# Expert weights cut by row blocks instead of by column halves, and the small group's two halves in one go

## The chip, the cores and the metric

The kernel runs on one core of one Trainium2 chip. The metric is the device time of one execution in microseconds, as the median of several runs. Five engines work side by side, each through its own queue in order: TensorE (PE in the profile; PEld is its weight load), VectorE (DVE), ScalarE (ACT), GpSimd (POOL) and SyncE (SP), which issues most DMAs here.

## The reference, cut to what matters

One transformer layer on 1024 tokens of width 1024: differential attention, then a mixture of experts, then a norm. The change lies in the experts. Each token chooses two of 16 experts; for every expert, with `t` the tokens routed to it:

```
hid = silu(t @ w_gate[e]) * (t @ w_up[e])      # w_gate, w_up: 1024 x 512
hid = hid * gates[:, e]
y  += hid @ w_down[e]                          # w_down: 512 x 1024
```

Everything is float32 in and out.

## The kernel before

**Precision.** Every float32 operand of the experts is split into a high part (fp32r, a cast on ScalarE) and a low part (float32 minus high part, a subtraction on VectorE). A product of a full block sums three terms: high x high, high x low and low x high (`TERMS`).

**Pieces of weights.** An expert has `NP = 12` pieces of 128 x 1024 float32 (512 KB): pieces 0 to 7 are gate (even) and up (odd), 8 to 11 are down. A piece of gate or up was four row blocks of 128 by half of the 512 columns. Half `hf` of the 512 hidden columns (256 each) so had its four pieces, `hf * 4` to `hf * 4 + 3`. `load_raw` issues the DMA of a piece into one of 11 raw tiles (`wraw`). `split_piece` does the cast `whi` (L1117) and the subtraction `wlo` (L1122) into a ring of 14 slots, so expert e + 1's piece i + 2 takes the slot of expert e's piece i.

**Order.** The order on TensorE, ScalarE, VectorE and GpSimd is written out by hand: instructions run in the order in which the program issues them. `block(e)` issues one expert. Its first 128 tokens are the full block: 48 gate and up products of half 0 (`gu`, 256 columns each), then 48 of half 1, counted 0 to 95. Between them stand hooks, `(count, what)`: a hook of count c is issued ahead of product c. `SPL` are the hooks that split pieces 6 to 11 of this expert; `later` holds what the expert before has postponed: its small group's last part at count `DSM` = 12, its output `yo` at 60. `gate` makes silu(gate) x up (L1397, L1398), `hid` transposes the result (L1404) and splits it (L1407, L1408), `down` multiplies it with the down pieces, 12 products of 512 columns for each half.

**The small group.** An expert with more than 128 tokens has a second group of up to `M2` = 64. Its work stands in branches, `small(...)`, that each engine takes or skips by the count of tokens; six of the experts (4, 6, 11 to 14) take them in this run. High and low parts lie side by side in one 128-row operand there, so a half takes 32 gate and up products and 8 down products. In order, after the full block's gate of half 1: the transposes of the group's tokens (L1292); full `down` of half 0 with the full block's second `hid` ("h1") in it; splits of pieces 0 and 1 of the next expert; small half 0 and its gate; splits 2 and 3; full `down` of half 1; then `small_c`: transposes and split of small half 0 (`hs`), small half 1 and its gate, small down products of half 0, transposes and split of small half 1; splits 4 and 5; and in the next block, at count 12, `small_d`: the small down products of half 1 (`spy`), the sum and the scatter.

**Block 0** has its own order of splits (`SP0`, and lines 1599 to 1622); there the low parts of pieces 3 and 4 are made by GpSimd. After expert 14 the last scatters and the final norm follow.

Of the kernel before, what the change touches and what calls it, by code (L numbers as in the profile page):

```python
# [4 lines left out]
F32 = mybir.dt.float32  # L5
F32R = mybir.dt.float32r
# [4 lines left out]
OP = mybir.AluOpType  # L11
# [4 lines left out]
P = 128  # L16
# [15 lines left out]
def f(ap):  # L32
    return ap.bitcast(F32)


def build(tc, x, c, ada_w, ada_b, norm_mix, norm_ffn, w_in, lq1, lk1, lq2, lk2, subln, w_out,
          rgw, rgb, rew, reb, wg, wu, wd, norm_final, out, dbg=None):
    nc = tc.nc
# [21 lines left out]
    ident = const.tile([P, P], F32, name="ident")  # L60
# [140 lines left out]
    for t in range(TB):  # L201
# [8 lines left out]
        for kk in range(2):  # L210
# [4 lines left out]
            for i in range(4):  # L215
                k = kk * 4 + i
# [806 lines left out]
    n = 5  # L1023
# [7 lines left out]
    for i, (h, qb) in enumerate(seq):  # L1031
# [6 lines left out]
        n = RATE.get(i, n)  # L1038
# [17 lines left out]
    WP = {}  # L1056
# [16 lines left out]
    M2 = 64  # L1073
# [10 lines left out]
    def load_raw(e, i):  # L1084

        raw = raw_tile()
        if HOLD[0]:

            nc.gpsimd.memset(raw[:, 0:1], 0.0)
        if i < 8:  # L1090
            src = (wg if i % 2 == 0 else wu)[0, e].rearrange("(k p) n -> p k n", p=P)
            hf, kk = i // 4, (i // 2) % 2
            nc.sync.dma_start(raw.rearrange("p (k n) -> p k n", k=4),
                              src[:, kk * 4:kk * 4 + 4, hf * 256:hf * 256 + 256])
        else:
            nc.sync.dma_start(raw, wd[0, e, (i - 8) * P:(i - 7) * P])
        RAW[e, i] = raw
# [39 lines left out]
    def split_to(n):  # L1137
        while nsplit[0] < min(n, NE * NP):
            split_piece(*divmod(nsplit[0], NP))
            split_done(1)  # L1140
# [5 lines left out]
    EVAC = 60  # L1146
    DSM = 12
    N0 = 28
    SPL = [(0, 6), (24, 7), (56, 8), (64, 9), (80, 10), (90, 11)]

    SP0 = [(20, split_hi, 8), (20, split_lo, 8), (30, split_hi, 9), (30, split_lo, 9), (40, split_hi, 10), (40, split_lo, 10),
           (45, split_hi, 11), (45, split_lo, 11)]
# [27 lines left out]
    mp = tc.alloc_tile_pool(name="moe", bufs=1, reuse_waits="tile")  # L1180
    mps = tc.alloc_tile_pool(name="moep", bufs=1, space=PSUM, reuse_waits="tile")

    v = nc.vector
# [117 lines left out]
    def run(g):  # L1301
        try:
            while True:
                next(g)
        except StopIteration as r:
            return r.value
# [68 lines left out]
    def gu_tile(tag="gu"):  # L1375
        return mps.tile([P, 2, 256], F32, name="gu", tag=tag, bufs=2 if tag == "gu" else 1)

    def gu(e, XT, hf, R, tag="gu", pg=None):
        pg = gu_tile(tag) if pg is None else pg
        for k in range(KT):  # L1380
            for xi, wi in TERMS[R]:
                for i in range(2):
                    yield
                    w = WP[e, hf * 4 + (k // 4) * 2 + i][wi].rearrange("p (k n) -> p k n", k=4)
                    nc.tensor.matmul(pg[:, i], XT[:, xi, k], w[:, k % 4], start=(k == 0 and xi == 0 and wi == 0 and i == 0),  # L1385
                                     stop=(k == KT - 1 and (xi, wi) == TERMS[R][-1] and i == 1), skip_group_check=True)
        return pg

    def gate(pg, g, R, lo=None, sl=None):

        sl = mp.tile([P, 256], F32, name="sl") if sl is None else sl
        if R == M2:
            lo = lo[:R].rearrange("p (i n) -> p i n", i=2)
            nc.scalar.copy(lo, pg[R:])
            v.tensor_tensor(lo, lo, pg[:R], op=OP.add)
            pg = lo
        nc.scalar.activation(sl[:R], pg[:R, 0], AF.Silu)  # L1397
        v.scalar_tensor_tensor(sl[:R], sl[:R], g[:R], pg[:R, 1], op0=OP.mult, op1=OP.mult)  # L1398
        return sl

    def hid(sl, R, name="hid", bufs=2, hT=None):
        ph = mps.tile([P, 2, P], F32, name="tp")
        for i in range(2):
            nc.tensor.transpose(ph[:, i, :R], sl[:R, i * P:(i + 1) * P], ident[:R, :R])  # L1404
        hT = mp.tile([P, 2, 2, P], F32R, name=name, bufs=bufs) if hT is None else hT
        hi, lo = (hT[:, 0, :, :R], hT[:, 0, :, R:]) if R == M2 else (hT[:, 0], hT[:, 1])
        nc.scalar.copy(hi, ph[:, :, :R])  # L1407
        v.tensor_tensor(lo, ph[:, :, :R], f(hi), op=OP.subtract)  # L1408
        return hT

    def down(e, py, hf, hT, R, ns=(0, 1)):
        terms = [(i, xi, wi) for i in range(2) for xi, wi in TERMS[R]]
        terms.sort(key=lambda t: t[1])
        for n in ns:
            for j, (i, xi, wi) in enumerate(terms):
                yield
                nc.tensor.matmul(py[n], hT[:, xi, i], WP[e, 8 + hf * 2 + i][wi][:, n * 512:(n + 1) * 512],  # L1417
                                 start=(hf == 0 and j == 0), stop=(hf == 1 and j == len(terms) - 1), skip_group_check=True)
# [72 lines left out]
    def block(e, XT, idx, tt, hooks):  # L1491


        count = [0]
        ix = idx[:, 0:1]
        last = e == NE - 1
        hooks = sorted(hooks, key=lambda hk: hk[0])
        py = [mps.tile([P, 512], F32, name="py%d" % i) for i in range(2)]

        def upto(c):  # L1500
            while hooks and hooks[0][0] <= c:
                hooks.pop(0)[1]()

        def go(g, n=1 << 30):
            try:
                for _ in range(n):
                    next(g)
                    upto(count[0])
                    count[0] += 1
            except StopIteration as r:  # L1510
                return r.value

        s0 = gate(go(gu(e, XT, 0, P)), tt[:, 0, 3:4], P)
        g1 = gu(e, XT, 1, P)
        go(g1, N0)
        h0 = hid(s0, P)
        pg1 = go(g1)
        if last:
            s1 = gate(pg1, tt[:, 0, 3:4], P)
            go(down(e, py, 0, h0, P))  # L1520
            h1 = hid(s1, P)
            nc.scalar.preload_act_table_set("natural_log_exp_and_others")  # L1522
            upto(1 << 30)
            run(down(e, py, 1, h1, P))
            finish15(ix, py, mp.tile([P, D], F32, name="yo"), XC[0])
            tc.no_sync_barrier()
            with tc.If(cnts[e] > P, label="small"):
                small15(XT, idx[:M2, 1:2], tt[:, 1, 3:4])
            tc.no_sync_barrier()
            with tc.If(cnts[NE] > P + M2):  # L1530
                rest(XT)
            return
        upto(199)
        n = cnts[e]
        g = tt[:, 1, 3:4]
        xs = XG[e, 1]

        def small(what):
            tc.no_sync_barrier()
            with tc.If(n > P):  # L1540
                what()

        def splits(k):
            split_to(nsplit[0] + k)

        s1 = gate(pg1, tt[:, 0, 3:4], P)
        pt = small_pt()
        small(lambda: small_evac(small_pe(xs, pt), XT))
        d = down(e, py, 0, h0, P)
        take(d, 9)  # L1550
        h1 = hid(s1, P)
        run(d)
        splits(2)
        sl, hs = mp.tile([P, 256], F32, name="sl"), mp.tile([P, 2, 2, P], F32R, name="hs")
        pg = gu_tile()
        small(lambda: gate(run(gu(e, XT, 0, M2, pg=pg)), g, M2, xs[:, 0:512], sl))
        splits(2)
        run(down(e, py, 1, h1, P))
        pg2 = gu_tile("idx")
        spy = [mps.tile([P, 512], F32, name="spy%d" % n, tag="xt", bufs=2) for n in range(2)]  # L1560

        def small_c():
            hid(sl, M2, hT=hs)
            gate(run(gu(e, XT, 1, M2, pg=pg2)), g, M2, xs[:, 512:1024], sl)
            run(down(e, spy, 0, hs, M2))
            hid(sl, M2, hT=hs)

        def small_d():
            for n in range(2):
                run(down(e, spy, 1, hs, M2, (n,)))  # L1570
                fold(spy, oyo, n)
                r = slice(n * 512, (n + 1) * 512)
                v.tensor_tensor(oyo[:M2, r], oyo[:M2, r], g2b[:M2, r], op=OP.mult)
            scatter_add(idx[:M2, 1:2], oyo[:M2])

        small(small_c)
        splits(2)
        later.append((DSM, lambda: small(small_d)))

        def evac():  # L1580
            yo = mp.tile([P, D], F32, name="yo")
            for n in range(2):
                v.tensor_tensor(yo[:, n * 512:(n + 1) * 512], py[n], g2b[:, n * 512:(n + 1) * 512], op=OP.mult)
            scatter_add(ix, yo)

        later.append((EVAC if e < NE - 2 else 0, evac))
        upto(1 << 30)
# [3 lines left out]
    g = nc.gpsimd  # L1591
    END = [*[(c, lambda: split_to(nsplit[0] + 1)) for c, i in SPL],
           *[(40, norm_load, t) for t in range(TB)], (40, rows15),
# [10 lines left out]
    XT = run(xpose(XG[0, 0]))  # L1604
# [22 lines left out]
    for e in range(NE):  # L1627
        idx, tt = ns[e]
# [42 lines left out]
        if 0 < e < NE - 1:  # L1671
            hooks += [(c, lambda: split_to(nsplit[0] + 1)) for c, i in SPL]
        if e == NE - 2:
# [7 lines left out]
        if e + 1 < NE:  # L1681
# [4 lines left out]
            XT = xp[0]  # L1686
# [34 lines left out]
```

## Time and profile before

| | us |
|---|---|
| median of 3 runs | 1222.99 (1222.16 to 1225.85) |
| the profiled execution's own time | 1222.66 |
| its span, first to last instruction | 1220.8 |
| mean granted TensorE clock | 0.961 |
| PE, DVE, ACT, POOL busy in the span | 1108.1, 939.6, 727.8, 265.2 |

The experts run from about 760 us on, expert 1 at 785, expert 2 at 807. How to read the rows below: a line of the timeline gives start and duration in us, the engine, the line of the kernel, the operation, what it writes and reads by the program's names, how many were merged into the row (x), and in brackets the idle time of the engine before it with what ended it. DVEq and ACTq are the engines' sequencers, L1540 is the skipped or taken branch.

### The profile page before, as it was taken

How to read it: one execution, taken by the hardware profiler on the slowest of the kernel's cores; microseconds unless marked ns; L12 is line 12 of the kernel's file. 1: busy time of each engine (PE TensorE's matmuls, PEld its weight loads, DVE VectorE, ACT ScalarE, POOL GpSimd, SP SyncE). 2: the span in 40 equal slices, each digit the busy share in tenths (PEclk: the TensorE clock that was granted, in tenths of full speed). 3: DMA queues.
4: the chain of work that ended last, by engine and by line, in shares of the span. 5: the costliest groups of instructions: out<-in, count | busy, mean ns of one | idle time of the engine just before them, and what ended most of it. 6: DMA issues, size and time to landing. Idle time of an engine off the chain costs nothing. (4 is left out here: it accounts for less than half of the span.)

```text
span 1220.8 us, 19162 instructions
## 1 busy us (share of the span) xinstructions
PE 1108.1 (91%) x6760; PEld 916.9 (75%) x6760; DVE 939.6 (77%) x1560; ACT 727.8 (60%) x1206; POOL 265.2 (22%) x283
## 2 busy tenths in 40 slices
PE   3889999999999999999889996999999999999961
PEld 3667777777777778787668885887888878888851
DVE  5869788888888777778884557798797989677754
ACT  5565766667666676776674323567465666554543
POOL 3011010111101011114304204343232332222121
PEclk9899999999999999999899996999999999999985
DMA  9722022322332110102417724799888999777645
GB/s 325 216 63 72 23 87 88 100 78 86 96 91 87 44 40 27 43 27 95 138 57 239 255 96 153 242 346 334 272 251 263 294 344 330 239 228 238 200 132 199
DMA packets 153255, 199.55 MB, mean 163 GB/s; under 512 B 12967, under 2 KB 124232, under 8 KB 153138
## 3 DMA queue, kind: packets, MB, share of 16 engines
q1 hardware_dynamic: 146432, 179.86, 45.0%
q0 software_dynamic: 6512, 17.68, 6.0%
q8 instruction: 63, 1.03, 0.4%
q10 hardware_dynamic: 194, 0.54, 0.1%
q14 instruction: 54, 0.44, 0.1%
HBM read 175.77 MB, written 27.67 MB: 167 GB/s over the span
## 5 line engine op out<-in xcount | busy, mean ns | idle before, releaser
L1122 DVE TENSOR_TENSOR wlo<-wraw,whi 128x1024 fp32r<-128x1024 f32 x187 | 224.9, 1231 | 33.2 <-ACT whi L1117 22.9
L1385 PE MATMUL gu<-whi,XT 128*128 128x256 f32 x1216 | 209.2, 284 | 2.7
L1117 ACT CAST whi<-wraw 128x1024 fp32r<-128x1024 f32 x192 | 193.4, 1049 | 6.4 <-ACTq L1540 4.7
L486 ACT ACTIVATE E<-E,mn 128x1024 f32<-128x1024 f32 x128 | 147.1, 1151 | 83.2 <-DVE mn L483 82.9
L1385 PEld LDWEIGHTS gu<-whi,XT 128*128 128x128 f32 x1216 | 172.3, 191 | 10.0 <-issue 5.8
L483 DVE CUSTOM_DVE_ANT_0 E<-S,negd 128x1024 f32<-128x1024 f32 x128 | 152.8, 1219 | 18.7 <-PE S L478 18.1
L1385 PE MATMUL gu<-wlo,XT 128*128 128x256 f32 x704 | 148.1, 289 | 2.0 <-POOL wlo L1122 2.0
L285 PE MATMUL mm<-hH,wh 128*128 128x512 f32 x336 | 139.3, 415 | 2.1 <-DVE V L384 2.1
L285 PE MATMUL mm<-hL,wh 128*128 128x512 f32 x336 | 140.2, 417 | 0.0
L285 PE MATMUL mm<-hH,wl 128*128 128x512 f32 x336 | 138.9, 413 | 0.0
L143 POOL TENSOR_TENSOR wl<-wraw,wh 128x1024 fp32r<-128x1024 f32 x21 | 50.6, 2410 | 325.3 <-ACT wh L142 255.3
L513 ACT CAST aH<-tp 128x512 fp32r<-128x512 f32 x128 | 74.0, 578 | 73.7 <-PE tp L511 73.5
L1385 PEld LDWEIGHTS gu<-wlo,XT 128*128 128x128 f32 x704 | 109.4, 191 | 2.4 <-POOL wlo L1122 2.2
L497 DVE SCALAR_TENSOR_TENSOR E<-E,r 128x1024 f32<-128x1024 f32 x64 | 85.8, 1341 | 27.9 <-ACT E L495 26.3
L514 DVE TENSOR_TENSOR aL<-tp,aH 128x512 fp32r<-128x512 f32 x128 | 88.0, 687 | 17.4 <-ACT aH L513 16.3
L1417 PE MATMUL py<-whi,hid 128*128 128x512 f32 x256 | 93.3, 426 | 3.2 <-ACT hid L1407 0.5
L511 PE MATMUL tp<-ident,E 128*128 128x128 f32 x512 | 79.2, 278 | 10.2 <-DVE aL L514 7.2
L511 PEld LDWEIGHTS tp<-ident,E 128*128 128x128 f32 x512 | 62.8, 142 | 33.5 <-DVE aL L514 13.9
L693 PE MATMUL mm<-wo,wh 128*128 128x512 f32 x240 | 80.1, 408 | 1.3 <-ACT mm L705 1.3
L285 PEld LDWEIGHTS mm<-hH,wh 128*128 128x128 f32 x336 | 63.5, 189 | 18.2 <-issue 5.1
L285 PEld LDWEIGHTS mm<-hH,wl 128*128 128x128 f32 x336 | 63.4, 189 | 17.1 <-issue 7.9
L285 PEld LDWEIGHTS mm<-hL,wh 128*128 128x128 f32 x336 | 63.3, 189 | 16.9 <-issue 8.0
(342 smaller groups left out, 2229.6 us busy)
## 6 DMA issues: line engine op xcount, KB each, us to landing
wraw<-in_expert_w_gate SPq DMA_DIRECT2D x64, 512.0 KB
wraw<-in_expert_w_up SPq DMA_DIRECT2D x64, 512.0 KB
wraw<-in_expert_w_down SPq DMA_DIRECT2D x64, 512.0 KB
aw<-in_ada_w SPq DMA_DIRECT2D x64, 256.0 KB
wraw<-in_attn_w_in SPq DMA_DIRECT2D x23, 512.0 KB
ld<-in_ada_w SPq DMA_DIRECT2D x32, 256.0 KB
ld<-in_x SPq DMA_DIRECT2D x8, 512.0 KB
xt<-in_x SPq DMA_DIRECT2D x8, 512.0 KB
```

The costliest lines, as they stand in the source:

```text
L285: nc.tensor.matmul(pq, w[:, k], t[k][:, n], start=(k == 0 and i == 0), stop=(k == KT - 1 and i == 2))
L483: nc.vector.tensor_tensor_reduce(out=e, in0=sps[m], in1=negd[:, w0:w0 + S], op0=OP.add, op1=OP.min, scale=-slope, scalar=3.0e38, accum_out=mn)
L486: nc.scalar.activation(e, e, AF.Exp, bias=mn, scale=-1.0, accum_out=sm)
L497: nc.vector.scalar_tensor_tensor(es[0], es[1], r2, es[0], op0=OP.mult, op1=OP.add)
L511: nc.tensor.transpose(pt[:, i], a[:, k * P:(k + 1) * P], ident)
L513: nc.scalar.copy(th[:, kk * 4:kk * 4 + 4, q], pt)
L514: nc.vector.tensor_tensor(tl[:, kk * 4:kk * 4 + 4, q], pt, f(th[:, kk * 4:kk * 4 + 4, q]), op=OP.subtract)
L693: nc.tensor.matmul(py, w[:, h], wt[h][:, ns], start=(h == 0 and s == 0), stop=(h == H - 1 and s == 2))
L1117: nc.scalar.copy(WP[e, i][0], RAW[e, i])
L1122: eng.tensor_tensor(low, RAW[e, i], f(high), op=OP.subtract)
L1385: nc.tensor.matmul(pg[:, i], XT[:, xi, k], w[:, k % 4], start=(k == 0 and xi == 0 and wi == 0 and i == 0), stop=(k == KT - 1 and (xi, wi) ...
L1417: nc.tensor.matmul(py[n], hT[:, xi, i], WP[e, 8 + hf * 2 + i][wi][:, n * 512:(n + 1) * 512], start=(hf == 0 and j == 0), stop=(hf == 1 and ...
```

## The change

A gate or up piece is now two row blocks of 128 by all 512 columns. Both halves of the gate and up products so read all eight pieces, two of them (gate and up) for each pair of row blocks. The hook that splits piece 7 moves from count 24 to count 8. In the small group, both halves of the gate and up products come one after the other, each in a branch of its own, with two splits between them and two behind them; the full `down` of half 1 and two more splits follow; `small_c` is now only four transposes with one cast and one subtraction; and all 16 small down products are in `small_d`. The gate's result is written into `xs`, in place, instead of a tile `sl`.

```diff
         if i < 8:
             src = (wg if i % 2 == 0 else wu)[0, e].rearrange("(k p) n -> p k n", p=P)
-            hf, kk = i // 4, (i // 2) % 2
-            nc.sync.dma_start(raw.rearrange("p (k n) -> p k n", k=4),
-                              src[:, kk * 4:kk * 4 + 4, hf * 256:hf * 256 + 256])
+            kk = i // 2 * 2
+            nc.sync.dma_start(raw.rearrange("p (k n) -> p k n", k=2), src[:, kk:kk + 2])
...
-    SPL = [(0, 6), (24, 7), (56, 8), (64, 9), (80, 10), (90, 11)]
+    SPL = [(0, 6), (8, 7), (56, 8), (64, 9), (80, 10), (90, 11)]
...
-                    w = WP[e, hf * 4 + (k // 4) * 2 + i][wi].rearrange("p (k n) -> p k n", k=4)
-                    nc.tensor.matmul(pg[:, i], XT[:, xi, k], w[:, k % 4], start=(k == 0 and xi == 0 and wi == 0 and i == 0),
+                    w = WP[e, k // 2 * 2 + i][wi].rearrange("p (k n) -> p k n", k=2)
+                    nc.tensor.matmul(pg[:, i], XT[:, xi, k], w[:, k % 2, hf * 256:hf * 256 + 256], start=(k == 0 and xi == 0 and wi == 0 and i == 0),
...
         run(d)
+        hs = mp.tile([P, 2, 2, P], F32R, name="hs")
+        pgs = [gu_tile(), gu_tile("idx")]
+
+        def small_b(hf):
+
+            gate(run(gu(e, XT, hf, M2, pg=pgs[hf])), g, M2, xs[:, hf * 512:hf * 512 + 512],
+                 xs[:, hf * 512:hf * 512 + 256])
+
+
+        small(lambda: small_b(0))
         splits(2)
-        sl, hs = mp.tile([P, 256], F32, name="sl"), mp.tile([P, 2, 2, P], F32R, name="hs")
-        pg = gu_tile()
-        small(lambda: gate(run(gu(e, XT, 0, M2, pg=pg)), g, M2, xs[:, 0:512], sl))
+        small(lambda: small_b(1))
         splits(2)
         run(down(e, py, 1, h1, P))
-        pg2 = gu_tile("idx")
+        splits(2)
         spy = [mps.tile([P, 512], F32, name="spy%d" % n, tag="xt", bufs=2) for n in range(2)]
 
         def small_c():
-            hid(sl, M2, hT=hs)
-            gate(run(gu(e, XT, 1, M2, pg=pg2)), g, M2, xs[:, 512:1024], sl)
-            run(down(e, spy, 0, hs, M2))
-            hid(sl, M2, hT=hs)
+            ph = mps.tile([P, 2, P], F32, name="tp").rearrange("p i (h n) -> p (i h) n", h=2)
+            for i in range(4):
+                c = (i // 2) * 512 + (i % 2) * P
+                nc.tensor.transpose(ph[:, i], xs[:M2, c:c + P], ident[:M2, :M2])
+            h = hs.rearrange("p h i n -> p (h i) n")
+            nc.scalar.copy(h[:, :, :M2], ph)
+            v.tensor_tensor(h[:, :, M2:], ph, f(h[:, :, :M2]), op=OP.subtract)
 
         def small_d():
             for n in range(2):
-                run(down(e, spy, 1, hs, M2, (n,)))
+                for hf in range(2):
+                    run(down(e, spy, hf, hs[:, hf:hf + 1], M2, (n,)))
                 fold(spy, oyo, n)
...
         small(small_c)
-        splits(2)
         later.append((DSM, lambda: small(small_d)))
```

## Rows read from the trace of the kernel before

**Rows 1.** The page: busy us, share of the span and instructions.
```profile
PE 1108.1 (91%) x6760; PEld 916.9 (75%) x6760; DVE 939.6 (77%) x1560; ACT 727.8 (60%) x1206; POOL 265.2 (22%) x283
```
**Rows 2.** Windows: length; PE, PEld, DVE, ACT, POOL busy; clock; DMA share; GB/s.
```profile
807.00:828.75 21.75, 20.31 (x148) 17.72 (x148) 19.50 (x29) 14.39 (x21) 7.42 (x10) 1.00 1.06 348
...
929.00:963.00 34.00, 32.24 (x222) 27.82 (x221) 24.91 (x40) 19.41 (x30) 7.44 (x11) 1.00 0.78 233
```
**Rows 3.** Timeline of VectorE, expert 1's tail and block 2.
```profile
803.33 0.42 DVE L1408 TENSOR_TENSOR hid<-tp,hid 128x256 fp32r<-128x256 f32 x1 [0.99 <-DVEq L1540]
804.27 2.36 DVE L1122 TENSOR_TENSOR wlo<-wraw,whi 128x1024 fp32r<-128x1024 f32 x2 [0.52 <-ACT whi L1117]
806.88 2.36 DVE L1122 TENSOR_TENSOR wlo<-wraw,whi 128x1024 fp32r<-128x1024 f32 x2 [0.24 <-DMA wraw<-in_expert_w_down]
809.48 3.50 DVE L1122 TENSOR_TENSOR wlo<-wraw,whi 128x1024 fp32r<-128x1024 f32 x3 [0.24 <-DVEq L1540]
813.22 1.23 DVE L1122 TENSOR_TENSOR wlo<-wraw,whi 128x1024 fp32r<-128x1024 f32 x1 [0.24 <-PE gu L1385]
814.36 0.48 DVE L1398 SCALAR_TENSOR_TENSOR sl<-sl,tt,gu 128x256 f32<-128x256 f32 x1
```
**Rows 4.** Timeline of TensorE, block 2.
```profile
807.08 0.47 PE L1385 MATMUL gu<-whi,XT 128*128 128x256 f32 x2
...
808.33 1.02 PE L1385 MATMUL gu<-whi,XT 128*128 128x256 f32 x4
...
824.14 0.44 PE L1404 MATMUL tp<-ident,sl 128*128 128x128 f32 x2 [0.76 <-DVEq L1540]
```
**Rows 5.** Timeline of ScalarE, block 2, expert 6's small group and block 7.
```profile
813.25 0.38 ACT L1397 ACTIVATE sl<-gu 128x256 f32<-128x256 f32 x1 [1.49 <-PE gu L1385]
...
929.96 0.58 ACT L1394 COPY xgxb<-gu 64x512 f32<-64x512 f32 x1 [2.39 <-issue]
...
947.46 0.39 ACT L1397 ACTIVATE sl<-gu 128x256 f32<-128x256 f32 x1 [2.48 <-PE gu L1385]
```
**Rows 6.** Timeline of TensorE, expert 6's small group and block 7.
```profile
939.35 0.31 PE L1404 MATMUL tp<-ident,sl 64*128 64x64 f32 x2 [0.57 <-DVE sl L1398]
939.60 0.51 PE L1385 MATMUL gu<-whi,XT 128*128 128x256 f32 x2
...
941.14 0.40 PE L1417 MATMUL spy<-whi,hs 128*128 128x512 f32 x1
...
943.00 0.40 PE L1385 MATMUL gu<-whi,XT 128*128 128x256 f32 x2
```
**Rows 7.** Timeline of VectorE, expert 6's small group and block 7.
```profile
930.58 0.68 DVE L1395 TENSOR_TENSOR xgxb<-xgxb,gu 64x512 f32<-64x512 f32 x1 [1.57 <-ACT xgxb L1394]
931.74 0.47 DVE L1398 SCALAR_TENSOR_TENSOR sl<-sl,tt,xgxb 64x256 f32<-64x256 f32 x1 [0.48 <-ACT sl L1397]
932.68 2.36 DVE L1122 TENSOR_TENSOR wlo<-wraw,whi 128x1024 fp32r<-128x1024 f32 x2 [0.46 <-PE py L1417]
...
948.26 0.47 DVE L1398 SCALAR_TENSOR_TENSOR sl<-sl,tt,gu 128x256 f32<-128x256 f32 x1
```
**Rows 8.** Groups by line and shape from 600 us on: busy, mean ns, idle before.
```profile
L1117 ACT CAST whi<-wraw 128x1024 fp32r<-128x1024 f32 x192 | 193.4, 1049 | 6.4 <-ACTq L1540 4.7 <-DMA wraw<-in_expert_w_gate 0.6 <-DMA wraw<-in_expert_w_up 0.4
```
**Rows 9.** Timeline, block 0.
```profile
767.37 2.37 POOL L1122 TENSOR_TENSOR wlo<-wraw,whi 128x1024 fp32r<-128x1024 f32 x1
...
769.79 0.50 PE L1385 MATMUL gu<-wlo,XT 128*128 128x256 f32 x2 [1.98 <-POOL wlo L1122]
```
**Rows 10.** Windows of TensorE alone: length, busy, clock, DMA share, GB/s.
```profile
770.90:774.20 3.30, 3.30 (x18) 0.50 1.00 319
...
866.50:869.80 3.30, 3.30 (x11) 0.50 1.04 278
...
921.40:925.00 3.60, 2.75 (x19) 1.00 1.14 316
```
**Rows 11.** Timeline of ScalarE and VectorE, expert 14's small group and its output.
```profile
1153.04 0.58 ACT L1394 COPY xgxb<-gu 64x512 f32<-64x512 f32 x1 [2.43 <-issue]
...
1166.44 1.28 DVE L1583 TENSOR_TENSOR yo<-py,g2b 128x512 f32<-128x512 f32 x2
```

## What I expected, written before the changed kernel was run

> **What bounds the kernel now.** I read the busy shares first [rows 1]. TensorE is busy 91% of the span and VectorE 77%, so at first sight TensorE is the bound and VectorE has room. The windows by expert say otherwise [rows 2]. A block whose expert has no second, small group of tokens ("skipped" below: 0 to 3, 5, 7 to 10) takes 21.75 us, and VectorE works 19.5 of them; a block with a small group (4, 6, 11 to 14) takes about 34 us, with 25 us of VectorE work. The reader is to see that the bound changes from block to block. Expert 15 has no small group.
>
> Then the order of time on VectorE in one skipped block [rows 3]. From the subtraction L1408 (h1, ends at 803.75) to the end of the eighth split (814.45) VectorE has only four short holes, 0.52 and three of 0.24 us, where the engines pass a skipped branch or wait for the cast of the first piece. The gate product L1398 follows at once, at 814.36. TensorE, meanwhile, waits 0.76 us for VectorE before the transposes L1404 of the next h1, at 824.14 [rows 4]. So in a skipped block the loop runs through VectorE: h1, eight splits, gate, the other splits, gate, h1.
>
> Now when the splits are needed. Before the change, half 0 of the gate and up products needs pieces 0 to 3 alone; pieces 4 and 5 are needed from product 48 and 6 and 7 from product 72 of a block. TensorE starts the block at 807.08 [rows 4] and ends half 0 at 813.25, where ScalarE's silu is released [rows 5]. That is before piece 7 is split, and TensorE does not have to care.
>
> In a small block TensorE is the bound. Its row shows a wait of 0.57 us before the second pair of small transposes (939.35), and the rest is one product behind another [rows 6].
>
> **The change part by part.** Bytes, casts, splits, matrix products and their tile shapes stay the same; runs in memory go from 1 to 2 KB, for which I count nothing, since casts waited 1.0 us for weights in 192 [rows 8]. What moves is the moment of need.
>
> Skipped blocks (blocks 1, 2, 3, 4, 6, 8, 9, 10, 11 follow a skipped expert). Half 0 now reads all eight pieces: 0 and 1 from product 0, 2 and 3 from 12, 4 and 5 from 24, 6 and 7 from 36; the low part of piece 7 is first read by product 39. The six splits behind h1 and the two in the next block run in the order of before, and the branches lie elsewhere: one ahead of the first split (up to 0.2 more, by the hole of a branch), and that of the postponed part now behind piece 7 (0.24 less). So piece 7 still ends at about 814.4. TensorE reaches product 39 earlier: start 807.08, 0.4 for one more branch (the four products at 808.33, where a branch is passed, took 1.02 us where 0.62 is due by the pace below, [rows 4]), 39 products of 0.117 (36 of them and the tail of the last took 943.00 to 947.46, [rows 5, 6]) and 0.4 for the branch at product 12: 812.5. It waits 1.9 us in all, in pieces. The nine products left and the tail take 1.3, so half 0 ends at 815.7 instead of 813.25: 2.45 late. Silu 0.38 and two hand-overs put the gate product at 816.15 instead of 814.36: VectorE, with nothing in between to do, loses 1.8. TensorE had 0.76 in hand at the transposes, and 2.45 less 1.8 is 0.65, so VectorE still closes the loop: 1.8 us for each of the six blocks whose own expert is skipped too. In blocks 4, 6 and 11 the small group comes next and TensorE carries on: 2.45 each. Sum 6 x 1.8 + 3 x 2.45 = 18.2. The bounds: nothing if piece 7 were ready at 812.5; 2.45 everywhere, 22.
>
> Blocks behind a small group (5, 7, 12, 13, 14; with the times of expert 6). Small half 0 ends at 929.96, where ScalarE's copy of it starts [rows 5]; the gate takes VectorE from 930.58 to 932.22 [rows 7]. Before, splits 0 and 1 lay ahead of this gate, in the time of the products; now all six lie behind it. Two splits: 932.68 to 935.04 [rows 7]. The 32 products of small half 1 follow half 0 at once and end at 933.7 (32 x 0.117), but its gate finds VectorE busy: branch 0.24, 935.28, and by the same 1.64 as for half 0 it ends at 936.92. Then, behind 0.46, four splits at 1.14 to 1.22 (three took 3.50, [rows 3]): 942.0; a branch, and the subtraction that makes hs (256 columns, 0.42 as L1408): 942.7. TensorE: small half 1 to 933.7, twelve down products (0.233 each: eight from 941.14 to 943.00, [rows 6]; 2.8) to 936.5, four transposes behind the gate to 937.5; the wait of 0.57 and the eight small down products (1.9) are gone from here, so the next block starts some 2 us earlier than 939.6. After twelve products, at 938.9, stands the postponed part, and its first product needs hs: a wait of 3.8 us, with the whole block queued behind it. Then 16 such down products to 946.4 and 36 products, 4.46, to 950.9 against 947.46: 3.4 late on TensorE; the gate at 951.3 against 948.26, 3.05 late on VectorE. Blocks 5 and 7 are followed by VectorE's loop, 3.05 each, 12 to 14 by TensorE's, 3.4 each: 16.3. Bounds: with hs in time the block would gain 0.4 (938.9 + 3.7 + 4.5 = 947.1); 3.4 everywhere, 17.
>
> Block 0. The low part of piece 4 is made by GpSimd from 767.37 to 769.74, and TensorE waits for it at product 50 [rows 9]. Now product 26 needs it: 24 products of half 0 move behind 769.79. 24 x 0.117 = 2.8, 5.6 at half clock; the stretch at half clock (770.9 to 774.2, [rows 10]) is there already, so 3.0.
>
> The end. The chain that ends last runs through the scatters of expert 14 and the norm behind them, and the first of these hangs on VectorE's yo, which stands right behind hs and splits 4 and 5. It started 13.4 us after the copy of small half 0 (1153.04 to 1166.44, [rows 11]); counted as for expert 6, hs ends 12.7 after that copy (929.96 to 942.7) and yo follows: -0.7. Block 15's products are not on this path.
>
> The clock. The granted clock was 0.50, the lower of its two levels (1.2 and 2.4 GHz), in 3.3 us that began 1.1 us after the 1.98 us wait of block 0, and in 3.3 us behind the first transposes of small group 4; at the same place of group 6 it stayed at 1.00, with TensorE idle 0.85 of 3.60 us [rows 10]. A wait of 3.8 is longer than all of these, so I charge the five of them. A stretch of 3.4 us at half clock costs up to 1.7 of work, less where part of it falls into the wait: 1.4 each, 7.0 (bounds 0 and 8.5). The waits of block 1 to 11 come in pieces of about a microsecond; I charge them nothing and keep 1.7 each for the upper end.
>
> Sum: 18.2 + 16.3 + 3.0 - 0.7 + 7.0 = 43.8 us. The profiled execution took 1222.66 us (span 1220.8 and 1.9 around it), within 0.4 of the median 1222.99. Forecast 1222.66 + 43.8 = 1266.5, say 1266.
>
> **A rule weighed.** The Trainium skill, Perfetto Trace Analysis, Identifying the Most-Contended Engine, takes occupancy as a fair measure of how near VectorE is to its limit. In a block with a small group VectorE has 25 of 34 us [rows 2], which by that rule is room, and the term of 16.3 would be nothing: 1250. The order of the rows speaks against it here: its work comes in a lump just where hs is due.
>
> **The rivals.** *hs in time.* The evacuation of the small transposes gets done before product 12, so the small blocks gain 0.4 each and no clock is lost: 1222.7 + 18.2 + 3.0 - 0.7 - 2.0 = 1241. For it: VectorE's room in these blocks. Against it: the order on ScalarE and VectorE is written out by hand, and four splits stand before hs.
>
> *The clock falls in all blocks.* Nine more times 1.7: 1266.5 + 15.3 = 1282. For it: group 4 lost the clock at a place where group 6, with the same work, did not [rows 10]. Against it: the skipped blocks with their 0.76 kept a clock of 1.00 [rows 2, 4].
>
> *Skipped blocks hold.* If the eight splits are ready when TensorE comes: 1266.5 - 18.2 = 1248. Against it: no hole in rows 3 from which 1.9 us could come.
>
> *The other side: the weights' arrival sets the pace.* In skipped blocks the DMA share is 1.06 at 348 GB/s [rows 2]. If pieces were cast as they land, longer runs would land them sooner, the splits would run ahead, and both waits vanish: -0.57 x 5 - 0.7 = 1219. Its place is the casts of pieces 0 to 7; it decides from the point where piece 7 is split 1.9 us and hs 3.8 us earlier than counted. Against it: 1.0 us of waiting for weights over 192 casts [rows 8].
> The Trainium skill, Perfetto Trace Analysis, DMA Optimizations, says that transfers under 2 KB pay a marked cost each and that larger ones can be much faster; this would be its effect here, 1219. The trace so far bears it out only in the full DMA share.
>
> **Chances.** Forecast 0.62, its own range 1254 to 1276; clock in all blocks 0.12; hs in time 0.13; skipped blocks hold 0.05; arrival 0.05; something unlisted 0.03. The range 1243 to 1283 leaves out the arrival case, part of the unlisted and the outer halves of the two nearest its ends, some 0.2. A difference of 0.3%, 3.7 us, is about what can be told from none. Slower 0.93; same 0.03 and faster 0.04 from the arrival case and the unlisted.
>
> **What would show it.** In the profile after: TensorE waiting for wlo inside half 0, at products 27, 38 and 39, in blocks 1 to 11, and VectorE idle near 1.8 us before L1398; TensorE waiting some 3.8 us for the small subtraction before the first spy product; half clock behind it; block 0 waiting for piece 4 from about 765 on. A skipped block would take 23.5 us in place of 21.75. I am wrong if VectorE reaches piece 7 earlier than 814.4 in this count, or if hs is evacuated ahead of splits 2 to 5.

## The result, and the profile after

The changed kernel takes 1270.48 us (median of four runs, 1267.13 to 1272.18), the one before 1224.42 beside it (four runs): ratio 1.0377, interval 1.0359 to 1.0394. That is 46.1 us slower, where 1266 and 43.8 had been forecast. The profiled execution of after has a span of 1270.3 us, 49.5 more than before, at a mean granted clock of 0.951 in place of 0.961.

The page of the kernel after, its line of engines [rows 1]:
```profile
PE 1128.5 (89%) x6760; PEld 931.5 (73%) x6760; DVE 942.0 (74%) x1554; ACT 726.1 (57%) x1200; POOL 269.0 (21%) x283
```
VectorE's work has grown by 2.4 us and TensorE's by 20, with the same number of products. The lower clock can account for some 15 of the 20 (0.049 of 1270.3 us is 62, 0.039 of 1220.8 is 48); the rest was not traced. What remains of the 49.5 us is idle time, and busy shares don't say where.

**A skipped block.** Windows of after, one skipped block and one with a small group (columns as in [rows 2]):
```profile
809.68:833.78 24.10, 21.05 (x148) 17.99 (x148) 19.59 (x28) 14.37 (x20) 7.47 (x11) 1.00 0.95 295
936.00:977.00 41.00, 36.43 (x240) 32.50 (x239) 25.51 (x39) 18.01 (x30) 9.27 (x11) 0.88 0.66 218
```
VectorE does the same 19.5 and 25 us of work as in [rows 2], in 24.1 and 41 us instead of 21.75 and 34. Where it stands still in the skipped block, its timeline after tells (answers to [rows 3]):
```profile
811.83 2.36 DVE L1121 TENSOR_TENSOR wlo<-wraw,whi 128x1024 fp32r<-128x1024 f32 x2 [0.73 <-ACT whi L1116]
814.43 4.63 DVE L1121 TENSOR_TENSOR wlo<-wraw,whi 128x1024 fp32r<-128x1024 f32 x4 [0.24 <-DMA wraw<-in_expert_w_down]
819.30 2.36 DVE L1121 TENSOR_TENSOR wlo<-wraw,whi 128x1024 fp32r<-128x1024 f32 x2 [0.24 <-DVEq L1539]
823.57 0.48 DVE L1397 SCALAR_TENSOR_TENSOR sl<-sl,tt,gu 128x256 f32<-128x256 f32 x1 [1.91 <-ACT sl L1396]
824.44 1.23 DVE L1121 TENSOR_TENSOR wlo<-wraw,whi 128x1024 fp32r<-128x1024 f32 x1 [0.39 <-DMA wraw<-in_expert_w_gate]
```
Line numbers of the helpers are one lower than before. The gate product L1397 once followed the eighth split at once; now there are 1.91 us of nothing between them. The split after it waits 0.39 more, and the first split 0.73 where [rows 3] has 0.52. TensorE and ScalarE in the same block, after:
```profile
819.12 0.39 PE L1384 MATMUL gu<-wlo,XT 128*128 128x256 f32 x1 [0.49 <-DVEq L1539]
...
821.72 0.38 PE L1384 MATMUL gu<-wlo,XT 128*128 128x256 f32 x1 [0.75 <-DVEq L1539]
...
833.82 0.44 PE L1403 MATMUL tp<-ident,sl 128*128 128x128 f32 x2 [0.74 <-DVEq L1539]
```
```profile
823.09 0.38 ACT L1396 ACTIVATE sl<-gu 128x256 f32<-128x256 f32 x1 [4.07 <-PE gu L1384]
823.37 1.99 ACT L1116 CAST whi<-wraw 128x1024 fp32r<-128x1024 f32 x2
```
TensorE waits inside half 0 for the low parts of pieces 5 and 7 (VectorE's rows above put the ends of these splits at 819.06 and 821.66), and still waits 0.74 us before the transposes of the next h1: VectorE closes the loop as before. The 0.39 comes from ScalarE's order: the first of the two casts behind the late silu ends near 824.4, and the split starts then. (The row names a DMA. At the same place of block 6, at 936.10, the profile names the cast.)

**A block with a small group.** VectorE and TensorE, expert 6's small group and the block after it:
```profile
961.24 4.63 DVE L1121 TENSOR_TENSOR wlo<-wraw,whi 128x1024 fp32r<-128x1024 f32 x4 [0.46 <-ACT whi L1116]
965.79 0.42 DVE L1576 TENSOR_TENSOR hs<-tp,hs 128x256 fp32r<-128x256 f32 x1
...
976.55 0.48 DVE L1397 SCALAR_TENSOR_TENSOR sl<-sl,tt,gu 128x256 f32<-128x256 f32 x1 [2.63 <-ACT sl L1396]
```
```profile
960.62 0.55 PE L1573 MATMUL tp<-ident,xgxb 64*128 64x64 f32 x4
...
966.35 0.47 PE L1416 MATMUL spy<-whi,hs 128*128 128x512 f32 x1 [3.57 <-ACT whi L1116]
...
968.28 0.63 PE L1416 MATMUL spy<-whi,hs 128*128 128x512 f32 x1
968.71 0.63 PE L1416 MATMUL spy<-wlo,hs 128*128 128x512 f32 x1
```
The transposes are done at 961.2. VectorE, which has to make hs from them, does four splits first, and TensorE stands still for 3.57 us with the whole next block behind the first of the 16 products. It is the same at all six small groups (3.56 to 3.61). Then a product of 512 columns takes 0.43 us (start to start) instead of 0.23. The group of these products, all six blocks, after:
```profile
L1416 PE MATMUL spy<-whi,hs 128*128 128x512 f32 x48 | 26.5, 553 | 21.5 <-ACT whi L1116 21.5
```
The idle 21.5 us are the six waits. (The releaser named, a cast, was long done; the product also needed hs, which ended at 966.2.) Windows of TensorE after, length, busy, clock, DMA share, GB/s:
```profile
880.20:883.60 3.40, 3.40 (x20) 1.00 0.97 269
899.20:905.90 6.70, 6.24 (x15) 0.51 1.02 331
943.60:950.30 6.70, 6.70 (x24) 0.51 0.84 272
967.40:970.70 3.30, 3.30 (x9) 0.50 1.05 382
```
Between block 0 and block 15 eight such stretches at the lower level (1.2 GHz) add up to 36.6 us by these windows; before there were three of 3.3. Six of the eight begin around the end of the wait for hs, from 0.7 us ahead of its end to 0.9 behind it. The two others lie behind the first small transposes of blocks 6 (943.60) and 13, where [rows 10] showed the loss for group 4; at that place in block 4 (880.20) the clock now holds.

**Block 0 and the end** (answers to [rows 9, 11]): the timelines of GpSimd and TensorE, and of ScalarE and VectorE at the output of expert 14; then a window of TensorE.
```profile
768.97 2.35 POOL L1121 TENSOR_TENSOR wlo<-wraw,whi 128x1024 fp32r<-128x1024 f32 x1
...
771.37 0.80 PE L1384 MATMUL gu<-wlo,XT 128*128 128x256 f32 x2 [4.69 <-POOL wlo L1121]
...
1203.70 0.58 ACT L1393 COPY xgxb<-gu 64x512 f32<-64x512 f32 x1 [4.18 <-PE gu L1384]
...
1215.67 1.28 DVE L1593 TENSOR_TENSOR yo<-py,g2b 128x512 f32<-128x512 f32 x2
```
```profile
771.40:776.40 5.00, 5.00 (x24) 0.53 0.73 275
```
TensorE now waits 4.69 us for piece 4 instead of 1.98, and does the products behind it at half clock. The output of expert 14 starts 12.0 us after the copy, 1.4 sooner than in [rows 11].
All of block 0 stands 1.6 us later than in [rows 9] already at the split of piece 4. There is no sign that the change does this: over the profiles of all kernels here the first gate and up product of block 0 came between 759.5 and 762.6 us, with the old cut at 759.6 to 762.2 and with the new one at 759.5 to 762.6.

### The profile page after: what moved, and what is told of

It is laid out like the page before. It is cut to its first block, busy times and chain, and to the rows that moved or that the text cites. A ratio compares the mean times of both kernels' runs of the same rounds, so it can differ in the third digit from the quotient of the medians.

```text
span 1270.3 us, 19295 instructions
## 1 busy us (share of the span) xinstructions
PE 1128.5 (89%) x6760; PEld 931.5 (73%) x6760; DVE 942.0 (74%) x1554; ACT 726.1 (57%) x1200; POOL 269.0 (21%) x283
## 5 line engine op out<-in xcount | busy, mean ns | idle before, releaser
L1384 PE MATMUL gu<-wlo,XT 128*128 128x256 f32 x704 | 154.7, 294 | 15.2 <-DVEq L1539 10.5
L497 DVE SCALAR_TENSOR_TENSOR E<-E,r 128x1024 f32<-128x1024 f32 x64 | 85.8, 1341 | 27.9 <-ACT E L495 26.3
L511 PEld LDWEIGHTS tp<-ident,E 128*128 128x128 f32 x512 | 62.3, 141 | 33.7 <-DVE aL L514 13.9
L285 PEld LDWEIGHTS mm<-hH,wh 128*128 128x128 f32 x336 | 63.6, 189 | 18.2 <-issue 5.1
```

Of the source, the lines that this page charges most:

```text
L285: nc.tensor.matmul(pq, w[:, k], t[k][:, n], start=(k == 0 and i == 0), stop=(k == KT - 1 and i == 2))
L497: nc.vector.scalar_tensor_tensor(es[0], es[1], r2, es[0], op0=OP.mult, op1=OP.add)
L511: nc.tensor.transpose(pt[:, i], a[:, k * P:(k + 1) * P], ident)
L1384: nc.tensor.matmul(pg[:, i], XT[:, xi, k], w[:, k % 2, hf * 256:hf * 256 + 256], start=(k == 0 and xi == 0 and wi == 0 and i == 0), stop=( ...
```

## The experiments

The theory: two independent causes. The **cut** makes half 0 need all eight splits, which VectorE has only when half 0 is nearly over; the **order** of the small group puts four splits ahead of hs, so TensorE stops and loses its clock. Rivals: the loads set the pace, or one of the two costs nothing. Each median stands beside that of the kernel before in the same runs (1223.0 to 1224.1).

| run | us | ratio (95% interval) |
|---|---|---|
| e1_order | 1251.28 | 1.0214 (1.0196 to 1.0232) |
| e2_hs_early | 1242.56 | 1.0148 (1.0132 to 1.0165) |
| e3_runs_1k | 1274.49 | 1.0414 (1.0396 to 1.0432) |
| e4_fill | 1244.96 | 1.0189 (1.0158 to 1.0219) |
| e5_new_cut_mended | 1225.57 | 1.0017 (1.0008 to 1.0026) |
| e6_fill_before | 1215.35 | 0.9935 (0.9921 to 0.9950) |
| e7_old_cut_one_branch | 1220.29 | 0.9968 (0.9958 to 0.9979) |
| e8_block0 | 1269.47 | 1.0371 (1.0356 to 1.0386) |
| e9_old_cut_all | 1213.26 | 0.9916 (0.9903 to 0.9930) |
| e10_evac_only | 1219.66 | 0.9970 (0.9959 to 0.9981) |
| e11_onehot_only | 1216.84 | 0.9945 (0.9932 to 0.9959) |
| e12_busy_wait | 1260.23 | 1.0295 (1.0281 to 1.0309) |

**e1_order: the old cut, with the new order of the small group.** The load and the products of gate and up are those of before, the rest is after.
```diff
-            kk = i // 2 * 2
-            nc.sync.dma_start(raw.rearrange("p (k n) -> p k n", k=2), src[:, kk:kk + 2])
+            hf, kk = i // 4, (i // 2) % 2
+            nc.sync.dma_start(raw.rearrange("p (k n) -> p k n", k=4),
+                              src[:, kk * 4:kk * 4 + 4, hf * 256:hf * 256 + 256])
...
```


> Changed kernel with the pieces cut as before (four row blocks by half of the columns), new order of the small group kept. My theory (need of all eight pieces in half 0 costs the skipped blocks and block 0; the late hs costs the blocks behind a small group): the gate-to-gate time of a skipped block falls from 24.05 to 21.9 us, TensorE's long wait for piece 4 in block 0 goes, but the 3.6 us wait before the first spy product and the half clock behind it stay: about 1247 us, some 23 above before. Rival (the cut alone costs; the new order is neutral or a gain): 1224 or a little less. Rival (arrival of weights sets the pace): no faster than 1270.


27.2 us slower than before, 4 more than expected; the cut is worth the other 19. The skipped blocks are back at 22.0 to 22.4 us from gate to gate, and the six waits for hs stay. Two causes, but not quite each in its own blocks: before, the skipped blocks took 21.6 to 22.0 us, so that the new order (with piece 7's hook at count 8, which no run moved alone) costs 3.8 us over these nine. That is about the 4 that were not expected.

**e2_hs_early: the changed kernel with `small_c` ahead of the last four splits.**
```diff
-        splits(2)
         run(down(e, py, 1, h1, P))
-        splits(2)
...
         small(small_c)
+        splits(4)
```


> Changed kernel, with the branch that evacuates the small transposes (small_c) put ahead of the last four splits of the tail instead of behind them. My theory: hs is ready when the postponed part comes, so the wait of 3.6 us before spy and the half clock behind it go in five blocks (5 x (3.6 + 1.5 to 2) less a little for the later splits), skipped blocks stay at 24.05: about 1247 us. Rival (the splits are the bottleneck whichever comes first, so the wait only moves to the products that need pieces 2 to 7): 1265 to 1270.


27.9 us faster than after, some 4 more than expected. VectorE's and TensorE's timelines for expert 6 in this run:
```profile
952.94 0.42 DVE L1574 TENSOR_TENSOR hs<-tp,hs 128x256 fp32r<-128x256 f32 x1 [0.89 <-ACT hs L1573]
953.89 6.90 DVE L1121 TENSOR_TENSOR wlo<-wraw,whi 128x1024 fp32r<-128x1024 f32 x6 [0.52 <-ACT whi L1116]
```
```profile
953.90 0.40 PE L1416 MATMUL spy<-whi,hs 128*128 128x512 f32 x1
```
The subtraction now stands ahead of the splits, the product follows with no wait, and most skipped blocks keep their 24 us (two, behind small groups, take 23.4). So it was the order on VectorE, not its amount of work.

**e3_runs_1k: the changed kernel with each piece loaded by two DMAs of 1 KB runs.** Same bytes, same needs.
```diff
-            nc.sync.dma_start(raw.rearrange("p (k n) -> p k n", k=2), src[:, kk:kk + 2])
+            for hf in range(2):
+                nc.sync.dma_start(raw[:, hf * 512:hf * 512 + 512].rearrange("p (k n) -> p k n", k=2),
+                                  src[:, kk:kk + 2, hf * 256:hf * 256 + 256])
...
```


> Changed kernel with the same pieces loaded in runs of 1 KB, as before, by two DMAs of 256 KB for each gate or up piece. My theory (loads are ahead of their casts, run length counts nothing): 1270, within 0.3%. Rival (longer runs helped and hid part of the loss, arrival sets the pace): slower by 1% or more, 1283 and up, with casts waiting for DMA.


4 us slower than after, a little outside what was expected; the intervals of the two ratios just do not touch. The casts of weights in this run, and after:
```profile
L1118 ACT CAST whi<-wraw 128x1024 fp32r<-128x1024 f32 x192 | 191.6, 1047 | 7.6 <-DMA wraw<-in_expert_w_gate 3.2 <-ACTq L1541 3.0 <-DMA wraw<-in_expert_w_up 0.4
```
```profile
L1116 ACT CAST whi<-wraw 128x1024 fp32r<-128x1024 f32 x192 | 191.5, 1046 | 6.3 <-ACTq L1539 1.9 <-DMA wraw<-in_expert_w_down 1.5 <-DMA wraw<-in_expert_w_gate 1.3
```
Waiting for gate and up weights stays between 1 and 4 us in 192 casts. The loads don't set the pace. Whether the 4 us come from the shorter runs or from twice as many DMAs is open.

**e4_fill: the changed kernel with VectorE's other work moved into the hole.** The evacuation of the last output (yo, 1.3 us) and the one-hot work (1.5 us) come at count 14 instead of 60 and 66.
```diff
-    OH = 66
+    OH = 14
...
-    EVAC = 60
+    EVAC = 14
```


> Changed kernel with two pieces of VectorE's later work put into its hole before the gate product of half 0: the output product yo (1.28 us) from count 60 to 14 and the one-hot rows (1.6 us) from count 66 to 14. My theory (the 1.8 us in which VectorE has nothing to do close the loop of a skipped block): gate to gate 24.05 falls to about 22.2, nine blocks, so 1252 to 1257 us. Rival (the late half 0 on TensorE is itself the cost, whatever VectorE does meanwhile): 1270 or slower, since the gate then also comes later.


25.5 us faster than after, more than expected. VectorE in a skipped block of this run:
```profile
816.00 2.36 DVE L1121 TENSOR_TENSOR wlo<-wraw,whi 128x1024 fp32r<-128x1024 f32 x2 [0.24 <-DVEq L1539]
818.58 1.29 DVE L1593 TENSOR_TENSOR yo<-py,g2b 128x512 f32<-128x512 f32 x2 [0.21 <-DVEq L1539]
819.78 1.54 DVE L1230 TENSOR_SCALAR rk<-rk 128x192 bf16<-128x192 bf16 x8
821.24 0.46 DVE L1397 SCALAR_TENSOR_TENSOR sl<-sl,tt,gu 128x256 f32<-128x256 f32 x1
```
The hole of 1.91 us is full, and most skipped blocks take 22.4 to 23.1 us. TensorE's waits for low parts stay (0.46 and 0.75 in this block), its wait before the transposes is gone, so that now TensorE closes the loop. Idle time of VectorE ahead of the gate was thus part of the cost of the cut, but the 25.5 us are not the price of this hole: between the two profiled executions, 28.8 us apart, the nine skipped blocks give 7.1. The five blocks of experts 4, 6 and 11 to 13 give 18.0, though their waits for hs stay (3.56 to 3.62): VectorE had such a hole there too (2.63 at 976.55 above), and TensorE's eight stretches at half clock became four, all of the short kind.

**e6_fill_before: the same two numbers in the kernel before.** A control on e4.


> The kernel before, with yo and the one-hot rows moved to count 14 as in the run that filled the hole: a control. My theory: VectorE has no hole at this place in the kernel before, so nothing is gained: 1224, within 0.4%, or a little slower because the gate comes later. Rival (the earlier yo is a gain by itself, by earlier scatters or shorter queues): 1210 or less.


A miss: 8 us faster than before. **e10_evac_only** and **e11_onehot_only** move one of the two numbers each.


> The kernel before, with the evacuation of the last block's output alone moved from product 60 to product 14 of the block. Theory: in the skipped blocks VectorE sets the pace, and it loses 0.25 us of each period to short holes in front of the splits; either of the two moved pieces of work can lie there. This one is 1.4 us of VectorE's work and would give at most half of what both gave (1215.4 us): 1219 to 1221. Rival: the whole gain comes with the evacuation, since it also lets the scatter of the rows start sooner: 1215 to 1216. Other rival: it is the clock of the blocks with a small group alone, which one of the two moves brings and the other does not: then this one gives either 1215 to 1217 or no change.

> The kernel before, with the one-hot work for the expert after next alone moved from product 66 to product 14 of the block. Theory: as for the evacuation alone, about half of the gain of both: 1219 to 1221. Rivals: all of the gain (1215 to 1217), since the one-hot work stands ahead of the second gate product and makes the transposes of the next half wait; or none (1223 to 1225).


Either gives the same 21.50 us for a skipped block, 0.23 less than before, some 2 us in all. The rest hangs on the blocks of experts 4, 11 and 13. Before they took 1.6 us longer than those of 6, 12 and 14 (35.0 to 35.1 against 33.4 to 33.7) and held the three stretches at half clock. At the place of the stretch of [rows 10] in block 4, right behind the small transposes, e6 has
```profile
865.30:868.60 3.30, 3.30 (x19) 1.00 1.06 390
```
and e6 and e11 have no such long block left, e10 two of the three. So e10 comes out as expected and e11 as its rival had it, with most of the gain (ratio 0.9945 against 0.9970). Why the clock holds there stays open. TensorE's idle time ahead of these transposes in block 4 does not decide it; before, e6, and e11:
```profile
865.52 0.68 PE L1292 MATMUL xt<-ident,xgxb 64*128 64x64 f32 x8 [0.93 <-PE gu L1385]
...
864.31 0.68 PE L1292 MATMUL xt<-ident,xgxb 64*128 64x64 f32 x8 [0.30 <-PE gu L1385]
...
864.76 0.68 PE L1292 MATMUL xt<-ident,xgxb 64*128 64x64 f32 x8 [1.24 <-issue]
```
In e11 it is longer than before, and the clock holds all the same. Nor does half clock always cost the block: e11 keeps one stretch, behind the small transposes of block 13, and that block takes 33.6 us.
```profile
1106.90:1110.10 3.20, 3.20 (x8) 0.50 0.76 219
```

**e7_old_cut_one_branch, e9_old_cut_all and e5_new_cut_mended: versions.** e7 has the old cut, both small halves in one branch behind two splits, then `small_c`, then four splits. e9 is e7 with the two numbers of e4. e5 is e9 with the new cut (and with piece 7's hook at count 8 and piece 4 of block 0 split on VectorE). From the edit of e7 against the kernel before:
```diff
...
         splits(2)
-        sl, hs = mp.tile([P, 256], F32, name="sl"), mp.tile([P, 2, 2, P], F32R, name="hs")
-        pg = gu_tile()
-        small(lambda: gate(run(gu(e, XT, 0, M2, pg=pg)), g, M2, xs[:, 0:512], sl))
-        splits(2)
+
+        def small_both():
+            small_b(0)
+            small_b(1)
+
+        small(small_both)
         run(down(e, py, 1, h1, P))
...
         small(small_c)
-        splits(2)
+        splits(4)
```


> Old cut of the pieces, with the small group's two halves in one branch, splits 0 and 1 ahead of it, hs ahead of the last four splits, and piece 7 at count 24 as before. My theory: the order of the small group as such gains the 0.57 us wait and no more, if hs is in time: skipped blocks at 21.7 as before, blocks with a small group some 0.4 to 1 us shorter: 1219 to 1223. Rival (one evacuation for both halves and one run of products over both lets TensorE keep full clock): 1215 or less. Rival (later pieces 2 to 5 cost more than is gained): 1226 or more.

> New cut of the pieces, with all that the runs so far showed as mends: hs ahead of the last four splits, splits 0 and 1 ahead of the small group, both small halves in one branch, yo and the one-hot rows in VectorE's hole, and piece 4 of block 0 split by VectorE. My theory (the loss is made of the wait for pieces in half 0, the late hs and block 0, nothing else): skipped blocks at about 22.3 to 22.8 us, blocks with a small group at 33.5, block 0 like before: 1227 to 1233. Rival (the new cut costs something by itself, in the products or the loads): 1240 or more.

> The old cut of the pieces, with the small block's two halves in one branch and with the evacuation and the one-hot work moved from products 60 and 66 to product 14 (the sum of the two earlier kernels, 1220.3 and 1215.4 us). If the two gains lie in different places they add: -0.0032 and -0.0065 make a ratio near 0.990, 1212 us (range 1209 to 1215), skipped blocks 21.5 us, blocks with a small group 31.5 to 33. Rival: both take away the same stretches of half clock in the blocks with a small group, so that nothing adds: 1215 us, ratio 0.993 or 0.994.


e9 is the fastest here, 9.8 us faster than the kernel before; its interval overlaps that of e6, so that one of its parts adds to the other is likely but not shown. All products of one small group at once is a small gain once hs comes first (e7, 3.5 us, as expected). The new cut, with all covers in place, is 12 us behind the old one, though e5 came out 1.4 us better than the range expected for it: by the two traces some 5 in block 0 (see e8), 6 in the other skipped blocks (22.5 us against 21.56) and 3 in those with a small group.

**e8_block0: the changed kernel, piece 4 of block 0 split on VectorE instead of GpSimd.**
```diff
-        split_lo(0, 4, nc.gpsimd)
+        split_lo(0, 4)
```


> Changed kernel, with the low part of piece 4 in block 0 made by VectorE instead of GpSimd, nothing else. My theory: TensorE's wait of 4.7 us at product 26 of block 0 goes and with it the half clock behind: 1270 less 4 to 6: 1264 to 1266. Rival (another piece of block 0 is as late): 1269 to 1271.


A miss: some 5 us were expected, and the 1 us measured is no difference, since the intervals of the two ratios overlap. The wait for piece 4 is gone (the gate product starts at 770.31, not 776.86), but TensorE stops a little later. GpSimd and TensorE in this run:
```profile
765.82 3.49 POOL L1250 TENSOR_SCALAR tt<-ax,rk 128x2 f32<-128x2 f32 x1
769.27 1.17 POOL L1251 TENSOR_TENSOR tt<-ax 128x2 f32<-128x2 f32 x1
...
772.26 1.11 POOL L1262 DMA_INDIRECT xgxa<-h2d,ix  x1 [0.60 <-DVE rk L1230]
```
```profile
779.47 1.09 PE L1277 MATMUL xt<-ident,xgxa 128*128 128x128 f32 x4 [6.99 <-DMA xgxa<-h2d,ix]
```
The gather of expert 1's tokens is issued at 772.26, after at 767.03; GpSimd's small steps for its indices are slower here. The same wait, 5.68 us, stands in e5. Block 0 has two bounds close together, and taking one away brought out the other.

**e12_busy_wait: TensorE busy through the wait.** The changed kernel does 15 products that nothing needs, whose result is overwritten, ahead of the first small down product.
```diff
         def small_d():
+            for _ in range(15):
+                nc.tensor.matmul(spy[0], WP[e, 8][0][:, :P], WP[e, 8][0][:, :512], start=True, stop=True, skip_group_check=True)
             for n in range(2):
```


> The changed kernel, in which TensorE does 15 products of 128 by 512 (3.5 us) that nothing needs, ahead of the first of the 16 small down products, where it otherwise waits some 3.6 us for VectorE; their result is overwritten. Theory: the wait itself stays, but TensorE's clock does not fall behind it. The 16 products took 6.76, 5.51, 5.40, 6.77, 5.27 and 5.50 us in the six blocks, 35.2 together, and would take 3.72 each, 22.3: some 11 us less (the last of the six is not on the chain that ends last), 1258 to 1262, ratio near 1.029. Rivals: the half clock costs nothing, since a later wait of the block swallows it: 1270, ratio 1.0375; the clock falls all the same, so that the half clock is not due to this wait: 1270 or a little more.


10.2 us faster than after. In this run, TensorE's timeline at expert 6, the group of small down products, and the window of expert 6's 16 products:
```profile
956.76 3.60 PE L1580 MATMUL spy<-whi 128*128 128x512 f32 x15
960.41 0.47 PE L1416 MATMUL spy<-whi,hs 128*128 128x512 f32 x1
```
```profile
L1416 PE MATMUL spy<-whi,hs 128*128 128x512 f32 x48 | 19.4, 404 | 0.9 <-ACT whi L1116 0.5
```
```profile
960.40:964.30 3.90, 3.89 (x17) 1.00 1.01 361
```
The useful products start as late as after, 0.15 us behind the end of hs, but they run at full clock, 3.96 us for the 16. So the half clock was due to standing still, and it cost some 10 of the 46 us by itself.

## Why the prediction was right, step by step

The span grew by 49.5 us, 1.6 of them ahead of the experts. The others go by the time from one block's first gate product to the next one's.

| step of the prediction | predicted | measured |
|---|---|---|
| skipped blocks, on the gate (9 x 1.8) | 16.2 | 19.1 |
| small groups: 16.3, the clock's 7.0, and 2.0 left over from 18.2 | 25.3 | 25.3 |
| block 0 | 3.0 | 4.5 |
| the end | -0.7 | -1.0 |

**Skipped blocks: right in kind, a little small.** The eighth split and the closing wait of TensorE (0.74) came as counted, and VectorE's hole before the gate is 1.91 against 1.8. Nothing was counted for the casts on ScalarE behind the late silu (0.39), and the branches, "0.2 more" and "0.24 less", were set at nothing in sum, where the first split alone comes 0.21 later. Of the 19.1 us, 3.8 stay in e1 with the old cut: they belong to the new order. A block takes 23.9 to 24.1 us, not the 23.5 I gave. That the hole is part of it, e4 shows, which fills it and takes 7.1 of the 19.1 back; the rest of the sum is counted from the rows and was not tested piece by piece.

**Small groups: the wait is right (3.56 to 3.61 against 3.8), the sum right by luck, by errors that cancel.** The clock's "1.4 each" was too small: the 16 products took 35.2 us in the six blocks, and six times 3.96, 23.8, in e12 at full clock. That is 1.9 each, and 9.9 instead of 7.0 in the five blocks of the sum. The other terms, 16.3 and 2.0, were too large. In e12 the five blocks grew by 13.8; without the stretches behind the first small transposes (some 1.6 each; e12 has them in blocks 12 and 13, before had them in 4, 11 and 13) that makes about 15.5, between 2.9 and 3.2 for each block. Blocks behind a skipped one (4, 6, 11) grew no more than the others, so the 2.0 left over do not show. Third, the prediction left the half-clock stretches of before in the account, as if they stayed where they were. They moved: in blocks 4 and 11 they do not come again (880.20 above shows block 4), some 1.65 each, the 35.05 us of these blocks less the 33.4 of block 12. In block 6 a long one came (943.60), and hs's products start 31.1 us behind the gate there instead of 28. These two nearly cancel as well. I saw the loss of clock in [rows 10] as a price only, and not as time that a shifted schedule might give back or take elsewhere.

**Block 0: mis-sized.** "The stretch at half clock is there already, so 3.0": it was there, but in [rows 9, 10] it lay behind the gate (770.75), and now it lies on the products that the gate waits for. From 771.37 to the gate at 776.86 they take 5.5 us, which is the upper bound, 5.6, that I had put aside.

**The rivals.** "hs in time" needs hs ahead of the four splits, and e2 is that kernel: it gains 28 us. "Clock falls in all blocks" fell, since the skipped blocks kept 1.00. "Skipped blocks hold" fell with the 1.91. The weights' arrival fell with e3: runs of half the length, in place of a great loss, cost 0.4%. By the Trainium skill (Perfetto Trace Analysis, DMA Optimizations) transfers under 2 KB are dear. Here, with loads well ahead, that could at most be these 4 us. By the Trainium skill (Perfetto Trace Analysis, Identifying the Most-Contended Engine) occupancy is a fair measure of how near VectorE is to its limit. By that rule 1250 would have been possible. The trace does not agree: VectorE is busy 25.5 us of 41 in the small block after, and TensorE waited for it all the same.

## What to carry to other kernels

When the cut of an operand changes, write down for each consumer the last piece that it now needs and when the engine that makes the pieces gets there; the amount of work may be the same and the time not. In a hand-written order, look at what stands in front of the one small instruction that another engine waits for: four splits of 1.2 us ahead of a 0.4 us subtraction cost 28 us over six blocks. Work without a deadline is best put where an engine would stand still, and it is worth a try in the old kernel too, where it gave 8 us.

## What the runs showed of the hardware

TensorE's clock fell around the end of each of the six waits of 3.6 us, for 3.3 or 6.7 us, and a TensorE that did useless products through the same waits kept it there; that was worth 10.2 us (e12). Behind the small transposes half clock came and went between kernels and blocks, and no run here explains it.

GpSimd and VectorE were slower side by side: four splits on VectorE took 6.82 us after, while GpSimd made a split beside them, and 4.63 in e8, where it made none; there, beside VectorE's splits, one of GpSimd's 128 by 2 operations took 3.49 us (the row is in e8) in place of 0.34. VectorE after and in e8, and GpSimd after:
```profile
765.60 6.82 DVE L1121 TENSOR_TENSOR wlo<-wraw,whi 128x1024 fp32r<-128x1024 f32 x4
...
765.76 4.63 DVE L1121 TENSOR_TENSOR wlo<-wraw,whi 128x1024 fp32r<-128x1024 f32 x4
...
762.62 0.34 POOL L1250 TENSOR_SCALAR tt<-ax,rk 128x2 f32<-128x2 f32 x1
```
